# Strassen's method for part of two projections in a float32 encoder kernel on one core

## The chip, the core and the metric

The kernel runs on one core of a Trainium2 chip. Its engines are TensorE (PE in the rows; PEld is its weight load), VectorE (DVE), ScalarE (ACT), GpSimd (POOL) and SyncE (SP), which issues the DMAs. The metric is the device time of one execution in microseconds (us); 2767.62 us is the median of three runs of the kernel before.

## The reference

Two encoder layers on an input of 256 tokens by 2048 columns, in float32. Cut to what the change touches, a layer is:

```python
proj = x @ w_in                      # q, k, v of two attentions, then gate_A and gate_B, 2048 columns each
merged = sigmoid(ga) * (A @ w_pa) + sigmoid(gb) * (B @ w_pb)
x = layer_norm(alpha * x + merged @ w_out)
gate, up = split(x @ w_up)           # w_up is 2048 x 11264, gate and up have 5632 columns each
x = layer_norm(alpha * x + (silu(gate) * up) @ w_down)
```

## The kernel before

**Precision.** Every float32 operand of a large product is split into a high part that TensorE takes exactly and a low rest. ScalarE writes the high part (line 128, L290 for results), VectorE subtracts it to get the low part (L129, L291). A product of two blocks is then three matmuls: high by high (L215), high by low (L216), low by high (L217). All three have a 128 x 128 stationary operand, taken from the turned activations, and 512 moving columns of the weight.

**Tiles.** The 256 tokens are two row tiles t = 0, 1 of 128. The 2048 rows of `w_up` or of a gate are 16 tiles of 128, that is eight pairs. A *piece* is a pair of them by 512 columns (512 KB): one DMA into a `raw` buffer (six of these), one split on ScalarE and VectorE, and 2 row tiles x 2 weight tiles x 3 = 12 matmuls. A *chunk* of `w_up` is 512 gate columns and the 512 up columns that belong to them: eight pieces each, 16 in all, 192 matmuls; there are eleven chunks a layer. A chunk of the gates is 512 columns of gate_A and of gate_B; there are four a layer, each followed by its *merge*, two pieces of `w_pa` and four of `w_pb`.

**Order.** It is written out by hand; each engine runs its instructions in the order of the program. `run()` goes through the pieces. For piece m it first emits the splits up to piece m+3, then the matmuls of m, then what must follow them (`post`), then one item of a list, `background`:

```python
split_to(m + 1 + ahead)
...
pc["mm"](pc)
if pc["post"]:
    pc["post"]()
if background:
    background.pop(0)()
```

So an operation of VectorE that waits for the matmuls of piece m stands behind the splits up to m+3 and ahead of the split of m+4. After a chunk of `w_up`, ScalarE takes silu of the gate accumulator (L748), VectorE multiplies by the up accumulator (L752), and two background items turn the result with four transposes each (L402) and split it (L290, L291). The merge multiplies at L726 and L729 and adds at L730. `ln_turned` puts the loads and products of the layer norm's scale and shift (L436, L437) on the list as well.

**Memory.** An accumulator (`acc`) is two PSUM banks, one for each row tile; there are two, and four single banks (`aux`). Operands lie in 37 `units` of 4 KB a partition. `w_down` is taken in two parts, after chunks 0 to 5 and 6 to 10; the last 512 columns of its second part are done in two halves of 256 columns, for the layer norm that follows.

Of the kernel before, what the change touches and what calls it, by code (L numbers as in the profile page):

```python
# [14 lines left out]
ALU = mybir.AluOpType  # L15
# [61 lines left out]
def trunk(ctx: ExitStack, tc: tile.TileContext, x, rel_bias, w_in, sink, w_pa, w_pb, w_out,  # L77
# [27 lines left out]
    pieces = []  # L105
    background = []
    state = {"load": 0, "split": 0}
    norms = []

    def piece(src, kk, cc, mm, pre=None, post=None):  # L110
        pieces.append(dict(src=src, kk=kk, cc=cc, mm=mm, pre=pre, post=post))
        return pieces[-1]

    def load_to(m):
        while state["load"] < min(m, len(pieces)):
            pc = pieces[state["load"]]
            pc["raw"] = work.tile([P, pc["kk"], pc["cc"]], F32, name="raw", tag="raw", bufs=N_RAW)
            nc.sync.dma_start(pc["raw"], pc["src"])
            state["load"] += 1

    def split_to(m):
        while state["split"] < min(m, len(pieces)):
            load_to(state["split"] + 1 + AHEAD_LOAD)
            pc = pieces[state["split"]]
            raw = pc["raw"]
            hi = unit([P, pc["kk"], pc["cc"]], F32R, "whi")
            lo = unit([P, pc["kk"], pc["cc"]], F32R, "wlo")
            nc.scalar.activation(hi, raw, AF.Copy)  # L128
            nc.vector.tensor_tensor(out=lo, in0=raw, in1=hi.bitcast(F32), op=ALU.subtract)  # L129
            pc["hi"], pc["lo"] = hi, lo  # L130
            state["split"] += 1
# [118 lines left out]
    def gemm_a_halves(w, k0, k1, c0, width, xs, post, between):  # L250
# [398 lines left out]
    def layer(l, xt, pre, turn, after_last):  # L649
# [74 lines left out]
        def merge(c):  # L724
# [123 lines left out]
```

## Time and profile before

| | |
|---|---|
| median of three runs | 2767.62 us |
| the profiled execution | 2767.28 us, of which the span of its instructions is 2765.5 us |
| TensorE busy | 2749.0 us, 99% of the span, 13539 matmuls |
| VectorE busy | 1480.9 us, 54% |
| ScalarE busy | 1168.2 us, 42% |
| DMA | 531.84 MB, mean 192 GB/s |

Busy times of engines overlap one another. A matmul's end is modelled, so consecutive matmuls overlap in the records; how fast TensorE goes is read from the distance of their starts.

### The profile page before, as it was taken

To read this page: it belongs to the slowest core of one execution; us is meant where nothing else is said; L and a number is where in the kernel's file an instruction comes from. 1 tells how busy PE (TensorE), PEld (TensorE's weight loads), DVE (VectorE), ACT (ScalarE), POOL (GpSimd) and SP (SyncE) were. 2 spreads that over 40 slices of the span, in tenths; PEclk is the share of its full clock that TensorE was granted. 3 is DMA by queue.
4 is the path that set the end of the run, shared out by engine and by line. 5 is a ranking of instruction groups with operands and counts; after the bars stand their busy time and mean duration, and the time that the engine had idled before them with its cause. 6 is when DMAs were issued, how large, how long until landed. Compare 5 with 4: busy or idle time off the path is not lost.

```text
span 2765.5 us, 34763 instructions
## 1 busy us (share of the span) xinstructions
PE 2749.0 (99%) x13539; PEld 2319.5 (84%) x13539; DVE 1480.9 (54%) x1688; ACT 1168.2 (42%) x1407; POOL 5.4 (0%) x13
## 2 busy tenths in 40 slices
PE   9999999999999999999999999999999999999998
PEld 7888888888888888888889888888888888888887
DVE  5566554566644544445566655455665444444445
ACT  4454443444333443434344544433544344423441
POOL 0000000000000000000000000000000000000000
PEclk9999999999999999999999999999999999999999
DMA  8866665564655554655656666555645565555554
GB/s 255 241 183 181 185 202 178 187 229 149 225 184 183 208 204 158 211 177 191 215 162 201 179 183 191 177 201 179 232 162 198 183 205 205 183 183 183 187 209 145
DMA packets 359801, 531.84 MB, mean 192 GB/s; under 512 B 52288, under 2 KB 153664, under 8 KB 359636
## 3 DMA queue, kind: packets, MB, share of 16 engines
q1 hardware_dynamic: 358836, 528.31, 58.1%
q8 instruction: 106, 1.74, 0.3%
q10 hardware_dynamic: 800, 1.31, 0.1%
q14 instruction: 59, 0.48, 0.0%
HBM read 522.86 MB, written 6.68 MB: 191 GB/s over the span
## 4 chain that ended last, share of the span: by engine, by line
PE 98%; DVE 1%; DMA 0%; SPq 0%; issue 0%; ACT 0%; DVEq 0%; POOL 0%; ACTq 0%; POOLq 0%
PE acc L217 27%; PE acc L215 27%; PE acc L216 27%; PE acc L202 9%; PE acc L171 5%; PE aux L402 1%; PE aux L297 0%; PE aux L296 0%; PE aux L295 0%; DVE xT L392 0%; PE aux L562 0%; PE aux L528 0%; PE aux L620 0%; PE aux L544 0%; DMA res<-in_x_dram 0%; PE aux L370 0%
## 5 line engine op out<-in xcount | busy, mean ns | idle before, releaser
L129 DVE TENSOR_TENSOR wlo<-raw,whi 128x1024 fp32r<-128x1024 f32 x960 | 1127.4, 1221 | 474.5 <-ACT whi L128 455.4
L128 ACT ACTIVATE whi<-raw 128x1024 fp32r<-128x1024 f32 x960 | 971.5, 1054 | 434.9 <-DMA raw<-in_w_down_dram 142.1
L215 PE MATMUL acc<-whi,xT 128*128 128x512 f32 (+1 forms) x2176 | 848.7, 390 | 0.0
L217 PE MATMUL acc<-whi,xT 128*128 128x512 f32 (+1 forms) x2176 | 842.0, 387 | 0.0
L216 PE MATMUL acc<-wlo,xT 128*128 128x512 f32 (+1 forms) x2176 | 840.8, 386 | 0.0
L217 PEld LDWEIGHTS acc<-whi,xT 128*128 128x128 f32 x2176 | 409.1, 188 | 84.2
L215 PEld LDWEIGHTS acc<-whi,xT 128*128 128x128 f32 x2176 | 409.3, 188 | 80.8 <-issue 0.7
L216 PEld LDWEIGHTS acc<-wlo,xT 128*128 128x128 f32 x2176 | 409.4, 188 | 80.5
L202 PE MATMUL acc<-xT,whi 128*128 128x512 f32 x1088 | 387.0, 399 | 0.0
L171 PE MATMUL acc<-xT,wlo 128*128 128x256 f32 x1088 | 299.6, 280 | 0.0
L215 PE MATMUL acc<-whi,hT 128*128 128x512 f32 (+1 forms) x784 | 288.9, 368 | 0.0
L217 PE MATMUL acc<-whi,hT 128*128 128x512 f32 (+1 forms) x784 | 288.2, 368 | 0.0
L216 PE MATMUL acc<-wlo,hT 128*128 128x512 f32 (+1 forms) x784 | 288.0, 367 | 0.0
L202 PEld LDWEIGHTS acc<-xT,whi 128*128 128x128 f32 x1088 | 203.0, 188 | 43.3
L171 PEld LDWEIGHTS acc<-xT,wlo 128*128 128x128 f32 x1088 | 205.6, 189 | 2.6
L215 PEld LDWEIGHTS acc<-whi,hT 128*128 128x128 f32 x784 | 147.8, 189 | 24.3
L216 PEld LDWEIGHTS acc<-wlo,hT 128*128 128x128 f32 x784 | 147.9, 189 | 24.3
L217 PEld LDWEIGHTS acc<-whi,hT 128*128 128x128 f32 x784 | 147.8, 189 | 24.3
L290 ACT ACTIVATE hT<-aux 128x512 fp32r<-128x512 f32 x44 | 26.3, 598 | 315.2 <-PE aux L402 315.2
L752 DVE TENSOR_TENSOR sg<-sg,acc 128x1024 f32<-128x1024 f32 x22 | 26.9, 1221 | 202.3 <-PE acc L217 202.3
L215 PE MATMUL acc<-whi,mT 128*128 128x512 f32 (+1 forms) x320 | 111.5, 348 | 0.0
L217 PE MATMUL acc<-whi,mT 128*128 128x512 f32 (+1 forms) x320 | 111.0, 347 | 0.0
(133 smaller groups left out, 1503.8 us busy)
## 6 DMA issues: line engine op xcount, KB each, us to landing
raw<-in_w_up_dram SPq DMA_DIRECT2D x352, 512.0 KB, 4.7
raw<-in_w_in_dram SPq DMA_DIRECT2D x320, 512.0 KB, 4.9
raw<-in_w_down_dram SPq DMA_DIRECT2D x176, 512.0 KB, 5.5
raw<-in_w_out_dram SPq DMA_DIRECT2D x64, 512.0 KB, 5.6
raw<-in_w_pb_dram SPq DMA_DIRECT2D x32, 512.0 KB, 5.0
raw<-in_w_pa_dram SPq DMA_DIRECT2D x16, 512.0 KB, 5.9
bias<-ftab SPq DMA_DIRECT2D x96, 64.0 KB, 3.7
ftab<-fb SPq DMA_DIRECT2D x7, 640.0 KB
```

Source lines behind the costliest of these rows:

```text
L128: nc.scalar.activation(hi, raw, AF.Copy)
L129: nc.vector.tensor_tensor(out=lo, in0=raw, in1=hi.bitcast(F32), op=ALU.subtract)
L171: nc.tensor.matmul(st["acc"][:, n, 0:SEQ], lhsT=lo[:, k, n * P:(n + 1) * P], rhs=xs(4 * j + k)[:, 0, :], start=False, stop=False)
L202: nc.tensor.matmul(acc, lhsT=hi[:, k, n * P:(n + 1) * P], rhs=xs(kt).rearrange("p h t -> p (h t)"), start=first and not turn, stop=last)
L215: nc.tensor.matmul(o, lhsT=xk[:, 0, ts], rhs=hi, start=first, stop=False)
L216: nc.tensor.matmul(o, lhsT=xk[:, 0, ts], rhs=lo, start=False, stop=False)
L217: nc.tensor.matmul(o, lhsT=xk[:, 1, ts], rhs=hi, start=False, stop=last)
L290: nc.scalar.activation(hi, src, AF.Copy)
L402: nc.tensor.transpose(out=ps[:, k, t * P:(t + 1) * P], in_=src[:, t, c0:c0 + P], identity=ident)
L752: nc.vector.tensor_tensor(out=s, in0=s, in1=acc, op=ALU.mult)
```

## The change

**Two products at a time.** `gemm_s` computes two column blocks c1 and c2 of 512 (gate and up; or gate_A and gate_B) together. The eight pairs of weight tiles go by `PLAN = "SCSCSCCC"`. A *plain step* C is two pieces, one for each column block, with 24 matmuls as before. A *Strassen step* S takes the same two `raw` tiles (2 weight tiles x 2 column blocks, for 2 row tiles) with seven block products in place of eight, so 21 matmuls, in four pieces, of which the last two load nothing:

- S.1: split of the left tile; products q1 and q2 (6 matmuls)
- S.2: first sum of weight blocks (half of `t13`), split of one block of the right tile (`b22`); product q3 (3)
- S.3: second half of `t13`, first half of `t24`, split of `t13`, second half of `t24`; products q5 and q7 (6)
- S.4: split of `t24`; products q6 and q4 (6)

q2, q3, q4 and x share the two accumulators with the plain steps; q1, q5, q6, q7 take the four `aux` banks. After the third S, `fold()` combines those four into `e` and `f` (one copy on ScalarE, four operations on VectorE). In the last plain step VectorE adds `e` or `f` to each of the four banks as it is finished (L389), and silu, sigmoid and the product then read these sums (L927, L928 for `w_up`).

**Sums of activations.** `sum_rows` makes the sums of activation blocks that the S steps need, for three tiles of two, once for the gates and once for `w_up`, on VectorE with one copy on ScalarE.

**Where.** Chunks 1 to 10 of `w_up` and 1 to 3 of the gates, 26 chunks in both layers; chunk 0 stays as it was and makes room for the sums. Transposes now wait on a list of their own, `soon`, of which S steps and the plain steps up to the one behind the third S take nothing. `w_down` is taken in three parts, after chunks 0 to 3, 4 to 7 and 8 to 10.

```diff
+SUMS = 3
+PLAN = "SCSCSCCC"
...
+    soon = []
...
+            if pc["src"] is not None:
+                pc["raw"] = work.tile([P, pc["kk"], pc["cc"]], F32, name="raw", tag="raw", bufs=N_RAW)
+                nc.sync.dma_start(pc["raw"], pc["src"])
...
+            pc["split"](pc)
...
-            if background:
-                background.pop(0)()
+            if not pc.get("quiet") and (soon or background):
+                (soon or background).pop(0)()
...
+    def gemm_s(w, c1, c2, xs, sums, post, plan=PLAN):
...
+        def bank(n):
+            if "even" not in st:
+                st["even"], st["odd"] = acc_tile(), acc_tile()
+                st.update(q2=st["even"][:, 0, :], q3=st["even"][:, 1, :], q4=st["odd"][:, 0, :], x=st["odd"][:, 1, :])
+            if n not in st:
+                st[n] = aux_tile()
+            return st[n]
...
+            def split2(pc):
+                raw = b["right"] = pc["raw"]
+                b["t13"] = unit([P, 2, 512], F32, "t13")
+                nc.vector.tensor_tensor(out=b["t13"][:, 0, :], in0=b["left"][:, 0, :], in1=raw[:, 0, :], op=ALU.add)
+                b["b22"] = unit([P, 2, 512], F32R, "b22")
+                split_into(b["b22"][:, 0, :], b["b22"][:, 1, :], raw[:, 1, :])
...
+            def split3(pc):
+                b["t24"] = unit([P, 2, 512], F32, "t24")
+                for o, x0, x1 in ((b["t13"][:, 1, :], b["right"][:, 0, :], b["right"][:, 1, :]),
+                                  (b["t24"][:, 0, :], b["t13"][:, 0, :], b["right"][:, 1, :])):
+                    nc.vector.tensor_tensor(out=o, in0=x0, in1=x1, op=ALU.add)
+                b["h13"] = halves(b["t13"])
+                nc.vector.tensor_tensor(out=b["t24"][:, 1, :], in0=b["t24"][:, 0, :], in1=b["left"][:, 1, :], op=ALU.add)
+
+            def split4(pc):
+                b["h24"] = halves(b["t24"])
...
+        def fold():
+
+            e, f, d = unit([P, 2, 512], F32, "e"), unit([P, 2, 512], F32, "f"), work.tile([P, 512], F32, name="tmp", tag="tmp", bufs=2)
+            nc.scalar.activation(e[:, 0, :], st["q1"], AF.Copy)
+            nc.vector.tensor_tensor(out=d, in0=e[:, 0, :], in1=st["q6"], op=ALU.subtract)
+            nc.vector.tensor_tensor(out=e[:, 1, :], in0=d, in1=st["q7"], op=ALU.subtract)
+            nc.vector.scalar_tensor_tensor(f[:, 0, :], st["q5"], -1.0, d, op0=ALU.mult, op1=ALU.subtract)
+            nc.vector.scalar_tensor_tensor(f[:, 1, :], st["q5"], -1.0, e[:, 1, :], op0=ALU.mult, op1=ALU.subtract)
...
+                    if last:
+                        nc.vector.tensor_tensor(out=out_[:, t, :], in0=st[n], in1=st[extra][:, t, :], op=ALU.add)
...
+    def sum_rows(tile_):
...
+        nc.vector.tensor_tensor(out=a.rearrange("p (k t) -> p k t", k=2), in0=tile_[:, :, 0, :].bitcast(F32),
+                                in1=tile_[:, :, 1, :].bitcast(F32), op=ALU.add)
...
+        nc.vector.tensor_tensor(out=d[:, 0:2, :], in0=q[:, 1:4:2, :], in1=q[:, 0:2, :], op=ALU.subtract)
+        nc.vector.tensor_tensor(out=d[:, 2, :], in0=d[:, 1, :], in1=q[:, 0, :], op=ALU.add)
+        nc.vector.tensor_tensor(out=d[:, 3, :], in0=q[:, 2, :], in1=d[:, 2, :], op=ALU.subtract)
+        u = unit([P, 4, 2, P], F32R, "sT")
+        split_into(u[:, :, 0, :], u[:, :, 1, :], d)
...
-        background.extend([lambda: None, lambda: half(0), lambda: half(1)])
+        soon.extend([lambda: None, lambda: half(0), lambda: half(1)])
...
+                pieces[-6]["pre"] = lambda: (flush(), soon.extend([
+                    lambda i=i: xsums.append(sum_rows(xt[i])) for i in range(SUMS)]))
...
+        chunks = ((0, 4), (4, 8), (8, 11))
```

**What moves, first place: VectorE at the end of a chunk of `w_up`.** Before, around the product L752 that ends a chunk (tile numbers are those of the program):

```order
L129 TENSOR_TENSOR wlo_7138<-raw_7045,whi_7137 128x1024 [waits DVE_49,DMAHW0_49,PE_49,Activation_49]
L129 TENSOR_TENSOR wlo_7156<-raw_7063,whi_7155 128x1024 [waits DVE_49,DMAHW1_49,PE_49,Activation_49]
L752 TENSOR_TENSOR sg_7024<-sg_7024,acc_7032 128x1024 [waits PE_49]
L129 TENSOR_TENSOR wlo_7175<-raw_7081,whi_7174 128x1024 [waits DMAHW2_49,DVE_49,Activation_49]
L291 TENSOR_TENSOR hT_7196<-aux_7191,hT_7196 128x2x256 [waits Activation_49]
L129 TENSOR_TENSOR wlo_7202<-raw_7099,whi_7201 128x1024 [waits DMAHW3_49,Activation_49]
L291 TENSOR_TENSOR hT_7222<-aux_7217,hT_7222 128x2x256 [waits Activation_49]
```

Now, from the second half of the transposes of the chunk before, `hT`, to the product L928, where the next chunk begins with an S step too (`acc_8135` holds q2 and q3, `acc_8136` q4 and x):

```order
L443 TENSOR_TENSOR hT_8435<-aux_8430,hT_8435 128x2x256 [waits Activation_49]
L329 TENSOR_TENSOR t13_8440<-raw_8322,raw_8334 128x512 [waits DMAHW0_49]
L443 TENSOR_TENSOR b22_8442<-raw_8334,b22_8442 128x512 [waits Activation_49]
L389 TENSOR_TENSOR sg_8445<-acc_8135,e_8346 128x512 [waits PE_49]
L389 TENSOR_TENSOR sg_8445<-acc_8136,e_8346 128x512 [waits PE_49]
L342 TENSOR_TENSOR t13_8440<-raw_8334 128x512
L342 TENSOR_TENSOR t24_8462<-t13_8440,raw_8334 128x512 [waits DVE_49]
L443 TENSOR_TENSOR tlo_8466<-t13_8440,thi_8465 128x1024 [waits Activation_49]
L344 TENSOR_TENSOR t24_8462<-t24_8462,raw_8322 128x512 [waits DVE_49]
L389 TENSOR_TENSOR sg_8470<-acc_8135,f_8347 128x512 [waits PE_49]
L389 TENSOR_TENSOR sg_8470<-acc_8136,f_8347 128x512 [waits PE_49]
L928 TENSOR_TENSOR sg_8445<-sg_8445,sg_8470 128x1024 [waits DVE_49,Activation_49]
```

One operation that read the accumulator became five, and the sums and splits of the next chunk's S.2 and S.3 stand between them; the split of S.4 follows behind L928.

**Second place: TensorE at the same point.** Before, the first matmul of the next accumulator waited for ScalarE's split and for a release that lay far back:

```order
L215 MATMUL acc_6869<-whi_6954,xT_5502 128x512
L216 MATMUL acc_6869<-wlo_6955,xT_5502 128x512
L217 MATMUL acc_6869<-whi_6954,xT_5502 128x512
L215 MATMUL acc_7032<-whi_6972,xT_5495 128x512 [waits PE_49,Activation_49]
L216 MATMUL acc_7032<-wlo_6973,xT_5495 128x512 [waits DVE_49]
```

Now, from the last plain piece of a chunk to the first products of the next (its accumulator is `acc_8491`):

```order
L304 MATMUL acc_8135<-whi_8388,xT_5664 128x512 [waits DVE_49,Activation_49]
L305 MATMUL acc_8135<-wlo_8389,xT_5664 128x512
...
L304 MATMUL acc_8136<-whi_8388,xT_5664 128x512 [waits DVE_49]
L305 MATMUL acc_8136<-wlo_8389,xT_5664 128x512
...
L304 MATMUL aux_8493<-whi_8414,xT_5657 128x512 [waits Activation_49]
...
L304 MATMUL acc_8491<-whi_8414,xT_5657 128x512 [waits DVE_49]
```

By the counts in the program, the first wait is for VectorE's sum of q2 (the first L389 above), the second for its sum of q4, and the last, that of the next chunk's q2, for the sum of q3 (the third L389), since banks are released by whole tiles.

**Third place: VectorE in the merge of the gates' chunk 0**, from the split of the third-last piece on, before:

```order
L129 TENSOR_TENSOR wlo_3410<-raw_3314,whi_3409 128x1024
L726 TENSOR_TENSOR sg_3194<-sg_3194,acc_3394 128x1024
L129 TENSOR_TENSOR wlo_3429<-raw_3332,whi_3428 128x1024
L129 TENSOR_TENSOR wlo_3448<-raw_3350,whi_3447 128x1024
L129 TENSOR_TENSOR wlo_3466<-raw_3368,whi_3465 128x1024
L129 TENSOR_TENSOR wlo_3484<-raw_3388,whi_3483 128x1024
L729 TENSOR_TENSOR sg_3386<-sg_3386,acc_3432 128x1024
L730 TENSOR_TENSOR sg_3194<-sg_3194,sg_3386 128x1024
```

Now the second of the three `sum_rows` stands behind the product, and the third behind the next split:

```order
L443 TENSOR_TENSOR wlo_3414<-raw_3314,whi_3413 128x1024
L878 TENSOR_TENSOR sg_3194<-sg_3194,acc_3392 128x1024
L417 TENSOR_TENSOR v_3430<-xT_172 128x512
L421 TENSOR_TENSOR v_3430<-v_3430 128x256
L422 TENSOR_TENSOR v_3430<-v_3430 128x128
L423 TENSOR_TENSOR v_3430<-v_3430 128x128
L443 TENSOR_TENSOR sT_3435<-v_3430,sT_3435 128x4x128
L443 TENSOR_TENSOR wlo_3441<-raw_3332,whi_3440 128x1024
L417 TENSOR_TENSOR v_3457<-xT_186 128x512
```

The first `sum_rows` stands ahead of this piece, behind the split of the merge's fourth piece; S.1 to S.3 of the gates' chunk 1 follow the third.

## Rows read from the trace of the kernel before

**Rows 1.** The page, part 1: busy time, share of the span, instructions.

```profile
PE 2749.0 (99%) x13539; PEld 2319.5 (84%) x13539; DVE 1480.9 (54%) x1688; ACT 1168.2 (42%) x1407; POOL 5.4 (0%) x13
```

**Rows 2.** What TensorE waited for: us in total, times, longest.

```profile
PE aux L370 <- DMA res<-in_x_dram: 3.3, 2, 2.3
PE aux L377 <- DVE res L426: 1.5, 3, 0.5
```

**Rows 3.** Timeline of ScalarE (start, us): silu of two consecutive chunks of w_up.

```profile
808.48 1.03 ACT L748 ACTIVATE sg<-acc 128x1024 f32<-128x1024 f32 x1 [10.09 <-PE acc L217]
852.97 1.03 ACT L748 ACTIVATE sg<-acc 128x1024 f32<-128x1024 f32 x1 [10.09 <-PE acc L217]
```

**Rows 4.** Busy times in the 44.49 us between those two.

```profile
808.54:853.03 44.49, 44.49 (x202) 36.81 (x201) 21.13 (x19) 17.72 (x20) 0.00 (x0) 1.00 0.58 189
```

**Rows 5.** Timeline of TensorE: first and last of 22 consecutive matmuls, 512 columns.

```profile
804.65 0.39 PE L217 MATMUL acc<-whi,xT 128*128 128x512 f32 x1
...
809.41 0.39 PE L217 MATMUL acc<-whi,xT 128*128 128x512 f32 x1
```

**Rows 6.** The same: first and last of 19, 256 columns, in w_down.

```profile
2735.83 0.28 PE L217 MATMUL acc<-whi,hT 128*128 128x256 f32 x1
...
2737.99 0.28 PE L217 MATMUL acc<-whi,hT 128*128 128x256 f32 x1
```

**Rows 7.** Timeline of VectorE: runs of operations, 1024 and 512 columns.

```profile
721.50 8.04 DVE L129 TENSOR_TENSOR wlo<-raw,whi 128x1024 fp32r<-128x1024 f32 x7 [0.26 <-ACT whi L128]
...
686.34 0.69 DVE L436 TENSOR_TENSOR res<-res,gb 128x512 f32<-128x512 f32 x1
687.06 0.69 DVE L437 TENSOR_TENSOR res<-res,gb 128x512 f32<-128x512 f32 x1
687.68 2.35 DVE L129 TENSOR_TENSOR wlo<-raw,whi 128x1024 fp32r<-128x1024 f32 x2
```

**Rows 8.** Timeline, hand-overs: VectorE to ScalarE; TensorE, ScalarE, VectorE; VectorE to TensorE.

```profile
169.47 0.69 DVE L680 SCALAR_TENSOR_TENSOR tmp<-acc,tmp 128x512 f32<-128x512 f32 x1 [0.93 <-ACT tmp L281]
170.19 0.63 ACT L290 ACTIVATE parts<-tmp 128x512 fp32r<-128x512 f32 x1 [0.76 <-DVE tmp L680]
...
743.78 0.60 PE L402 MATMUL aux<-ident,sg 128*128 128x128 f32 x4
744.47 0.60 ACT L290 ACTIVATE hT<-aux 128x512 fp32r<-128x512 f32 x1 [12.34 <-PE aux L402]
745.10 0.69 DVE L291 TENSOR_TENSOR hT<-aux,hT 128x512 fp32r<-128x512 f32 x1 [1.49 <-ACT hT L290]
...
654.40 1.45 DVE L426 TENSOR_SCALAR res<-res,mv,rstd 128x512 f32<-128x512 f32 x3
655.09 0.52 PE L377 MATMUL aux<-ident,res 128*128 128x128 f32 x3 [0.49 <-DVE res L426]
```

**Rows 9.** Groups by line and shape: count, busy us, mean ns, idle before.

```profile
L128 ACT ACTIVATE whi<-raw 128x1024 fp32r<-128x1024 f32 x960 | 971.5, 1054 | 434.9 <-DMA raw<-in_w_down_dram 142.1 <-DMA raw<-in_w_up_dram 94.2 <-PE acc L217 66.3
L426 DVE TENSOR_SCALAR res<-res,mv,rstd 128x512 f32<-128x512 f32 x18 | 9.0, 543 | 0.1
L392 DVE TENSOR_TENSOR xT<-v,xT 128x256 fp32r<-128x256 f32 x30 | 12.8, 426 | 1.0
L392 DVE TENSOR_TENSOR xT<-v,xT 128x128 fp32r<-128x128 f32 x12 | 3.5, 292 | 0.4
```

**Rows 10.** Timeline around the merge of a gates' chunk: a split; the merge's end.

```profile
483.99 1.23 DVE L129 TENSOR_TENSOR wlo<-raw,whi 128x1024 fp32r<-128x1024 f32 x1 [11.39 <-ACT whi L128]
...
498.11 0.39 PE L215 MATMUL acc<-whi,xT 128*128 128x512 f32 x1
498.31 1.22 DVE L729 TENSOR_TENSOR sg<-sg,acc 128x1024 f32<-128x1024 f32 x1 [5.12 <-PE acc L217]
```

**Rows 11.** Two stretches near the start, columns as Rows 4; the eighth value is TensorE's granted clock.

```profile
9.00:12.00 3.00, 1.84 (x8) 1.45 (x9) 1.83 (x2) 1.28 (x3) 0.00 (x0) 0.83 1.05 330
12.00:16.00 4.00, 4.00 (x16) 3.20 (x15) 3.05 (x3) 1.91 (x3) 0.00 (x0) 0.70 1.06 286
```

More of the change, by code (lines that the diff above doesn't have):

```diff
@@ L110, in piece @@
     def piece(src, kk, cc, mm, pre=None, post=None):
-        pieces.append(dict(src=src, kk=kk, cc=cc, mm=mm, pre=pre, post=post))
+        pieces.append(dict(src=src, kk=kk, cc=cc, mm=mm, pre=pre, post=post, split=split_plain))
         return pieces[-1]
@@ L116, in load_to, with split_plain @@
             pc = pieces[state["load"]]
-            pc["raw"] = work.tile([P, pc["kk"], pc["cc"]], F32, name="raw", tag="raw", bufs=N_RAW)
-            nc.sync.dma_start(pc["raw"], pc["src"])
+            if pc["src"] is not None:
+                pc["raw"] = work.tile([P, pc["kk"], pc["cc"]], F32, name="raw", tag="raw", bufs=N_RAW)
+                nc.sync.dma_start(pc["raw"], pc["src"])
             state["load"] += 1
+    def split_plain(pc):
+        raw = pc["raw"]
+        pc["hi"] = unit(list(raw.shape), F32R, "whi")
+        pc["lo"] = unit(list(raw.shape), F32R, "wlo")
+        split_into(pc["hi"], pc["lo"], raw)
     def split_to(m):
@@ L124, in split_to @@
             pc = pieces[state["split"]]
[L125 to L130, printed above, removed]
+            pc["split"](pc)
             state["split"] += 1
@@ L733, in merge, with both, post @@
             gemm_a(w_pb[l], 0, 8, 512 * c, 512, lambda kt: lookup(ob)(kt), post_b)
-        for c in range(4):
-            gate(c)
-            merge(c)
+        xsums = []
+        def both(c):
+            def post(a, b):
+                for nm, v in (("a", a), ("b", b)):
+                    nc.scalar.activation(v, v, AF.Sigmoid)
+                    sg[nm] = v
+            gemm_s(wi, GA + 512 * c, GB + 512 * c, xs, xsums, post)
+        for c in range(4):
+            if c == 0:
+                gate(c)
+                merge(c)
+                pieces[-6]["pre"] = lambda: (flush(), soon.extend([
+                    lambda i=i: xsums.append(sum_rows(xt[i])) for i in range(SUMS)]))
+            else:
+                both(c)
+                merge(c)
         stats1 = small.tile([P, 2, 5, 6], F32, name="stats", tag="stats", bufs=2)
@@ L756, in layer, with post_both @@
         after2, between2, ret = after_last(stats2)
-        for half, (c0, c1) in enumerate(((0, 6), (6, 11))):
+        sums = []
+        def post_both(gate_, up_):
+            nc.scalar.activation(gate_, gate_, AF.Silu)
+            nc.vector.tensor_tensor(out=gate_, in0=gate_, in1=up_, op=ALU.mult)
+            turn_block(gate_, hs, "hT")
+        chunks = ((0, 4), (4, 8), (8, 11))
+        for part, (c0, c1) in enumerate(chunks):
             for c in range(c0, c1):
                 st = {}
-                gemm_a(w_up[l], 0, KT, 512 * c, 512, x1s, lambda acc, st=st: post_gate(acc, st),
-                       turn=(turn1 if c == 0 else None))
+                if c > 0:
+                    gemm_s(w_up[l], 512 * c, D_FF + 512 * c, x1s, sums, post_both)
+                    continue
+                gemm_a(w_up[l], 0, KT, 512 * c, 512, x1s, lambda acc, st=st: post_gate(acc, st), turn=turn1)
                 gemm_a(w_up[l], 0, KT, D_FF + 512 * c, 512, x1s, lambda acc, st=st: post_up(acc, st))
-            residual_gemm(w_down[l], 4 * c0, 4 * c1, lookup(hs), ALPHA if half == 0 else None,
-                          None if half == 0 else stats2, after2, between2)
+                pieces[-12]["pre"] = lambda: background.__setitem__(slice(0, 0), [
+                    lambda i=i: sums.append(sum_rows(x1t[i])) for i in range(SUMS)])
+            last = part == len(chunks) - 1
+            residual_gemm(w_down[l], 4 * c0, 4 * c1, lookup(hs), ALPHA if part == 0 else None,
+                          stats2 if last else None, after2, between2)
         if l < DEPTH - 1:
```

77 lines of the change are left out of this document (added).

## The prediction

> **What bounds the kernel now.** I began with busy times. TensorE is busy 99% of the span, VectorE 54%, ScalarE 42% [rows 1], and the view of waits gives TensorE 4.8 us in all [rows 2]. So the time is the number of matmuls by their spacing. In TensorE's timeline 22 matmuls of 512 columns start within 4.76 us, hence 4.76 / 21 = 0.2267 us each [rows 5]; those of 256 columns take 2.16 / 18 = 0.120 us [rows 6]. A chunk of `w_up` lasts 44.49 us from silu to silu [rows 3]: 192 x 0.2267 = 43.52, and 0.97 for two groups of transposes (0.485 each). In that window VectorE works 21.13 us, ScalarE 17.72, and the granted clock is 1.00, the 2.4 GHz level [rows 4]. A matmul taken out is time gained, as long as VectorE can prepare operands at the new pace.
>
> **What is removed.** Each S step does 21 matmuls for 24, three S a chunk: 9 fewer in 26 chunks (10 of `w_up` and 3 of the gates in each layer), 234 x 0.2267 = 53.05 us. The last columns of `w_down` lose 192 matmuls of 256 columns for 96 of 512: 23.04 - 21.76 = 1.28. Together 54.3 us, 2.04 a chunk. The point that decides is thus 54.3 / 26 = 2.09 us of new waiting a chunk.
>
> **What is added on VectorE.** The prices: seven 1024-column operations in 8.04 us, the last of them 1.22 long, start (8.04 - 1.22) / 6 = 1.137 apart; independent ones of 512 columns start 0.62 apart (687.06 to 687.68; I use 0.61), 0.72 where the second reads the first's result (686.34 to 687.06) [rows 7]. An S step has three low parts of 1024, one of 512 and four sums of 512. Two of the low parts can't begin until a sum has gone to ScalarE and back: 0.69 for the sum, 0.03 to hand over (169.47 + 0.69 to 170.19 [rows 8]), 1.05 for the copy [rows 9], about 0.03 back (an estimate, from 744.47 + 0.60 to 745.10 [rows 8]), 1.81 us from a sum's start to its low part's. The longest path through an S and a C step on this engine is five spacings of 1024 (t24's low part, two of C, the next left tile, t13's low part), two of 512 and two round trips: 5 x 1.137 + 2 x 0.61 + 2 x 1.81 = 10.52 us. TensorE needs 45 x 0.2267 = 10.20 for the same. So VectorE falls 0.32 behind with each S-C pair, if it begins without a lead.
>
> **The end of a chunk that another S follows.** The order in the first place of the change puts sums between splits. I laid it out from zero = the last matmul of the fourth plain step. Transposes of the second half: TensorE's 0.485; their low part on VectorE 1.32 after their start (743.78 to 745.10 [rows 8]), say 1.33. From there by spacings: half of t13 1.94, b22 2.55, sum of q2 3.16 (ends 3.85), sum of q4 3.77, second half of t13 4.38, its low part 4.38 + 1.81 = 6.19, second half of t24 7.33, sum of q3 7.94 (ends 8.63), sum of x 8.55, L928 9.27, low part of t24 10.41 (ends 11.63). VectorE to TensorE takes 0.15 (654.94 to 655.09 [rows 8]). TensorE: the left last piece ends at 0.485 + 12 x 0.2267 = 3.21; the right one has to wait for the sum of q2 until 4.00 (**0.79**); it ends at 6.72, q1 at 7.40; q2 of the next chunk waits for the sum of q3 until 8.78 (**1.38**); S.2 and S.3 follow, and S.4 waits for the low part of t24 until 11.78 (**0.05**). Second and third S each lose the **0.32** (0.33) above. Sum 2.87 us, against 2.04 saved: such a chunk takes 42.46 + 2.87 = 45.33. There are seven such boundaries a layer (1-2, 2-3, 4-5, 5-6, 6-7, 8-9, 9-10): 14 x 2.87 = 40.2.
>
> **Other places.** The other 12 chunks end before a plain step or a merge: low part 1.33, a split 1.94, sum of q2 3.08, end 3.77 + 0.15, wait 0.71: 8.5 in all. In the six chunks of gates the second and third S lose 0.65 each chunk: 3.9; two entries behind a merge a layer 0.33 each: 1.3. Chunks of `w_up` behind `w_down` or chunk 0 come in with a lead, as VectorE has 2 x 1.137 = 2.3 of work for 5.4 us of a plain step: nothing. The loads and products of the layer norm stand between two chunks: 1.33 x 2 = 2.7.
>
> `sum_rows` in the merge: a sum of 512, 256 and two of 128 columns and a low part, in series, with two copies on ScalarE: about 3.45 us each (from 0.69, 0.426, 0.292 and 0.60 [rows 8, 9] with their hand-overs; an estimate). Three of them with five splits, the product L878 and the sums and low parts of S.1 to S.3 make a chain of 24.4 us on VectorE from the split that starts at 483.99. In the trace the last products of that merge begin at 498.11 [rows 10]; the S step's q1 would begin after 15 more matmuls (3.40) and needs its operands at 501.7. VectorE is there at 508.4 + 0.15: a wait of 6.8, 2 x 6.8 = 13.6. Hidden I take the third part of `w_down` (four more updates of the residual a layer: in those stretches VectorE has the 3 us of room a step named above; uncovered they would cost 8 x 0.69 = 5.5) and the DMAs (same number; six buffers of `raw` are a lead of some 11 us at 12 x 0.2267 = 2.72 us a piece, less where pieces load nothing).
>
> **Sum.** 40.2 + 8.5 + 3.9 + 1.3 + 2.7 + 13.6 = 70.2 us of waiting, less 54.3: +15.9. The profiled execution took 2767.28 (its median stands 0.34 above): **2783 us**, 0.6% slower.
>
> Bounds for the unknowns. The spacing of 512 columns on VectorE: 0.61 to 0.72 [rows 7]; were all sums 0.72, each boundary costs 8 x 0.11 = 0.9 more, +12. Hand-overs may be shorter than I allow: without the last one to TensorE (0.15) and the twelve of 0.03 in three S steps, a chunk loses 0.5 less, 14 x 0.5 = -7. `sum_rows`: 2.3 (spacings alone) to 3.9 each, -7 to +3. I take the middle values, since these rows are of the same operations.
>
> **A rule to weigh.** Rows 7 show an operation starting before the one ahead has ended (1.137 apart, 1.22 long). The Trainium skill, "VectorE: DVE Perf Modes", section "The DRAIN you can't avoid", says that the next operation does not start until the pipe is empty; the trace disagrees for this kernel's splits, and the page itself excepts operations that are not held. Rows 7 decide my sum. By the page's rule it would be the third rival's.
>
> **Rivals.**
>
> *VectorE keeps ahead and TensorE hardly waits* (the other side). Its mechanism: the lead. The splits stand four pieces ahead, 10.9 us of matmuls; if the plain steps C4 and C5 rebuild more than the 0.32 + 2.2 that a boundary spends, the sums don't come late. With no waits 2767.3 - 54.3 = 2713; with half of the 70.2, 2748. For it: 21.13 of 44.49 us busy [rows 4], some 42 afterwards (20 operations of 1.22, 25 of 0.69), still under the chunk. Against: the sum of q2 stands behind low parts that wait for transposes, whatever the lead. It decides under 2.09 us a chunk. Chance 0.05 for all, 0.17 for a gain that is partly kept (2725 to 2762).
>
> *The waits eat the gain and no more*: 1.1 less at each boundary (spacings of 0.55 would do it), 14 x 1.1 = 15.4, hence 2768. Chance 0.17.
>
> *VectorE's operations do not overlap where they differ from one another*: durations of 1.22 and 0.69 as spacings. The S-C path gets 5 x 0.083 + 2 x 0.08 = 0.58 longer, a boundary 0.9: 2.05 a chunk of `w_up`, 28.7; 3.5 + 3.5 for gates, 2.4 for `sum_rows`, 2 for the others: +40, **2823**. Rows 7 speak against it. Chance 0.06.
>
> *The clock falls.* After 3.3 us of waits at 9 to 10.5 us TensorE was granted 0.83, then 0.70 of full speed [rows 11]: 3.0 x 0.17 + 4.0 x 0.30 = 1.7 us lost. If the two waits of a boundary (2.2 us within 5) do it as well, 14 boundaries and three entries of the gates make 17 x 1.7 = 29: **2812**. Chance 0.10. The Trainium skill, "TensorE: Matmul & The Clock Gate", section "HAM oscillation — how this bites in real kernels", tells of kernels whose clock falls again and again with gaps in TensorE's work; rows 11 show one such fall, and no row here shows one in a stretch of short waits.
>
> **Numbers.** My forecast holds 0.45, between 2773 and 2798. A measurement of this kernel can tell about 0.2%, 5.5 us. Faster 0.22, same 0.17, slower 0.45 + 0.06 + 0.10 = 0.61. Range: leaving out 2823, 2713 and the lower half of the partial gain (0.06 + 0.05 + 0.08) gives 2748 to 2815.
>
> **What would show it.** The profile after should have TensorE's waits near 75 us, on VectorE: L389 at the ends of chunks, L443 `tlo` in S.4; silus of consecutive chunks 45.3 apart (42.5 without waits); a gap of about 7 us before the gates' chunk 1; matmuls 0.227 apart and a granted clock of 1.00 between. I am wrong if silus stand under 44.5 apart, if the waits name ScalarE or a DMA, or if the clock falls.

## The result

The changed kernel takes 2805.97 us (median of four runs, 2805.58 to 2806.83) against 2767.91 us for the kernel before on the same chips: a ratio of 1.014 with a 95% interval from 1.0127 to 1.0152. It is 38 us slower; the forecast was 16 us. The sign and the engine were right, the size was not.

The page of the kernel after, part 1 (compare [rows 1]):

```profile
PE 2728.2 (97%) x13209; PEld 2261.4 (81%) x13209; DVE 1973.7 (70%) x2432; ACT 1306.2 (47%) x1601; POOL 5.4 (0%) x13
```

What TensorE waited for in it (compare [rows 2]; columns: us in total, times, longest):

```profile
PE acc L304 <- DVE sg L389: 34.9, 36, 2.3
PE aux L305 <- DVE tlo L443: 10.3, 25, 1.9
PE aux L304 <- ACT thi L442: 2.9, 6, 0.9
```

TensorE has 330 matmuls fewer and waits for VectorE in the two places that were named: for the sums L389 at the end of a chunk, and for the low part `tlo` in S.4. No DMA stands among the new waits. ScalarE stands there with 2.9 us, and what it waits for is a sum of VectorE.

A chunk with an S chunk before and behind it, between two silus in ScalarE's timeline:

```profile
1020.22 1.04 ACT L927 ACTIVATE sg<-sg 128x1024 f32<-128x1024 f32 x1
1065.86 1.04 ACT L927 ACTIVATE sg<-sg 128x1024 f32<-128x1024 f32 x1
```

Busy times in that stretch (columns as in [rows 4]):

```profile
1020.22:1065.86 45.64, 43.83 (x193) 34.81 (x192) 38.62 (x45) 22.87 (x27) 0.00 (x0) 1.00 0.60 185
```

It takes 45.64 us, where it was 44.49 before [rows 3] and would be 42.46 without waits. VectorE is busy for 38.62 of these 45.64 us, so its busy time has room; the granted clock is 1.00. The stalls of this chunk stand in TensorE's timeline:

```profile
1017.18 0.39 PE L306 MATMUL acc<-whi,xT 128*128 128x512 f32 x1
1018.17 0.47 PE L304 MATMUL acc<-whi,xT 128*128 128x512 f32 x1 [0.60 <-DVE sg L389]
...
1021.46 0.39 PE L306 MATMUL aux<-whi,xT 128*128 128x512 f32 x1
1022.83 0.50 PE L304 MATMUL acc<-whi,xT 128*128 128x512 f32 x1 [0.98 <-DVE sg L389]
...
1036.00 0.39 PE L304 MATMUL aux<-thi,sT 128*128 128x512 f32 x1
1036.53 0.50 PE L305 MATMUL aux<-tlo,sT 128*128 128x512 f32 x1
1036.87 0.40 PE L306 MATMUL aux<-thi,sT 128*128 128x512 f32 x1
```

A stall is read from the distance of the starts, less 0.2267: the right last piece waits 0.99 - 0.23 = 0.76 for the sum of q2; q2 of the next chunk 1.37 - 0.23 = 1.14 for the sum of q3; S.4 0.53 - 0.23 = 0.30, and the matmul behind it starts 0.11 late too. The number in brackets is smaller by 0.16, since a matmul's modelled end lies 0.39 behind its start; the third stall has no bracket at all. So the view of waits, 58.8 us in all, tells too little: the span grew from 2765.5 to 2803.8 us, and 38.3 us more with 54.3 us of matmuls gone make 92.6 us of new stalls.

On VectorE, the operations of one S step and the C step behind it, in the same chunk:

```profile
1024.62 1.22 DVE L443 TENSOR_TENSOR tlo<-t,thi 128x1024 fp32r<-128x1024 f32 x1
1025.76 3.49 DVE L443 TENSOR_TENSOR wlo<-raw,whi 128x1024 fp32r<-128x1024 f32 x3
1029.16 0.69 DVE L329 TENSOR_TENSOR t<-raw 128x512 f32<-128x512 f32 x1
1029.77 0.69 DVE L443 TENSOR_TENSOR b<-raw,b 128x512 fp32r<-128x512 f32 x1
1030.37 0.69 DVE L342 TENSOR_TENSOR t<-raw 128x512 f32<-128x512 f32 x1
1030.97 0.69 DVE L342 TENSOR_TENSOR t<-t,raw 128x512 f32<-128x512 f32 x1
1032.24 1.23 DVE L443 TENSOR_TENSOR tlo<-t,thi 128x1024 fp32r<-128x1024 f32 x1 [0.58 <-ACT thi L442]
1033.38 0.68 DVE L344 TENSOR_TENSOR t<-t,raw 128x512 f32<-128x512 f32 x1
1035.25 1.22 DVE L443 TENSOR_TENSOR tlo<-t,thi 128x1024 fp32r<-128x1024 f32 x1 [1.19 <-ACT thi L442]
```

From t24's low part to the next one's: 35.25 - 24.62 = 10.63 us, and TensorE needs 10.20. The two round trips are 1030.37 to 1032.24 and 1033.38 to 1035.25, 1.87 each; VectorE sits idle in them for 0.58 and 1.19 us (the brackets).

### The profile page after: what moved, and what is told of

It is laid out like the page before. It is cut to its first block, busy times and chain, and to the rows that moved or that the text cites. A ratio compares the mean times of both kernels' runs of the same rounds, so it can differ in the third digit from the quotient of the medians.

```text
span 2803.8 us, 34938 instructions
## 1 busy us (share of the span) xinstructions
PE 2728.2 (97%) x13209; PEld 2261.4 (81%) x13209; DVE 1973.7 (70%) x2432; ACT 1306.2 (47%) x1601; POOL 5.4 (0%) x13
## 4 chain that ended last, share of the span: by engine, by line
PE 73%; DVE 16%; ACT 5%; issue 4%; DMA 1%; SPq 0%; DVEq 0%; ACTq 0%; POOL 0%; POOLq 0%
PE acc L220 12%; PE acc L222 12%; PE acc L221 12%; PE acc L207 9%; PE acc L304 6%; PE acc L306 6%; PE acc L305 6%; DVE wlo L443 5%; PE acc L176 5%; ACT thi L442 3%; DVE tlo L443 3%; DVE sg L389 1%; PE aux L305 1%; DVE t L344 1%; DVE t L342 1%
## 5 line engine op out<-in xcount | busy, mean ns | idle before, releaser
L443 DVE TENSOR_TENSOR wlo<-raw,whi 128x1024 fp32r<-128x1024 f32 x882 | 1036.8, 1220 | 121.5 <-ACT whi L442 119.9
L442 ACT ACTIVATE whi<-raw 128x1024 fp32r<-128x1024 f32 x882 | 890.4, 1051 | 261.5 <-DMA raw<-in_w_down_dram 108.9
L304 PE MATMUL acc<-whi,xT 128*128 128x512 f32 x1118 | 443.1, 396 | 34.9 <-DVE sg L389 34.9
L306 PE MATMUL acc<-whi,xT 128*128 128x512 f32 x1118 | 436.3, 390 | 0.0
L305 PE MATMUL acc<-wlo,xT 128*128 128x512 f32 x1118 | 435.6, 390 | 0.0
L442 ACT ACTIVATE thi<-t 128x1024 fp32r<-128x1024 f32 x156 | 165.5, 1061 | 501.2 <-DVE t L342 317.7
L304 PEld LDWEIGHTS acc<-whi,xT 128*128 128x128 f32 x1118 | 209.9, 188 | 91.1 <-DVE sg L389 25.1
L443 DVE TENSOR_TENSOR tlo<-t,thi 128x1024 fp32r<-128x1024 f32 x156 | 191.0, 1225 | 108.2 <-ACT thi L442 108.2
L306 PEld LDWEIGHTS acc<-whi,xT 128*128 128x128 f32 x1118 | 209.8, 188 | 45.1
L305 PEld LDWEIGHTS acc<-wlo,xT 128*128 128x128 f32 x1118 | 210.1, 188 | 41.9
L220 PE MATMUL acc<-whi,xT 128*128 128x512 f32 (+1 forms) x512 | 195.9, 383 | 0.9 <-ACT xT L442 0.9
L221 PE MATMUL acc<-wlo,xT 128*128 128x512 f32 (+1 forms) x512 | 193.2, 377 | 1.0 <-DVE wlo L443 1.0
L222 PE MATMUL acc<-whi,xT 128*128 128x512 f32 (+1 forms) x512 | 193.1, 377 | 0.6 <-DVE xT L443 0.6
```

The lines of the kernel that those rows point to most:

```text
L220: nc.tensor.matmul(o, lhsT=xk[:, 0, ts], rhs=hi, start=first, stop=False)
L221: nc.tensor.matmul(o, lhsT=xk[:, 0, ts], rhs=lo, start=False, stop=False)
L222: nc.tensor.matmul(o, lhsT=xk[:, 1, ts], rhs=hi, start=False, stop=last)
L304: nc.tensor.matmul(o, lhsT=xk[0], rhs=hi, start=first, stop=False)
L305: nc.tensor.matmul(o, lhsT=xk[0], rhs=lo, start=False, stop=False)
L306: nc.tensor.matmul(o, lhsT=xk[1], rhs=hi, start=False, stop=last)
```

## The experiments

Theory: TensorE waits because of the *order* of VectorE's operations (two round trips in series, sums behind them), not for want of room on the engine. Rivals: release of banks by whole tiles; waits that follow the method wherever its steps stand; stalls that the profile only makes up. All runs are compared with the kernel before on the same chip (2766.9 to 2768.0 us).

**One round trip in place of two (e1).** In S.3:

```diff
-                b["h13"] = halves(b["t13"])
                 nc.vector.tensor_tensor(out=b["t24"][:, 1, :], in0=b["t24"][:, 0, :], in1=b["left"][:, 1, :], op=ALU.add)
+                b["h13"] = halves(b["t13"])
```

> The second half of t24 is summed ahead of the split of t13, so an S step has one round trip through ScalarE on VectorE's path in place of two; the work is the same. Theory (TensorE waits because VectorE's order puts two round trips in series, 10.64 us for an S and a C step against 10.20 on TensorE): the pair falls to 10.64 - 1.87 = 8.8 us, the stalls of S.4 (0.42 each, some 55 of them) go, the sum of q3 comes about 0.6 earlier at the end of a chunk; 35 to 40 us less, about 2769. Rival (the waits come from banks released by whole tiles, or from DMA): the same stalls come back under another name, 2800 to 2806.

Measured: 2778.52 us, 1.0035 [1.0022, 1.0048] of before, 27 us less than the changed kernel. VectorE's timeline of that run:

```profile
1022.39 0.68 DVE L342 TENSOR_TENSOR t<-raw 128x512 f32<-128x512 f32 x1
1022.99 0.68 DVE L342 TENSOR_TENSOR t<-t,raw 128x512 f32<-128x512 f32 x1
1023.71 0.69 DVE L343 TENSOR_TENSOR t<-t,raw 128x512 f32<-128x512 f32 x1
1024.32 2.49 DVE L443 TENSOR_TENSOR tlo<-t,thi 128x1024 fp32r<-128x1024 f32 x2
1026.73 3.49 DVE L443 TENSOR_TENSOR wlo<-raw,whi 128x1024 fp32r<-128x1024 f32 x3
```

Both low parts now follow one another without idle time, and a pair takes 8.95 us (1024.32 to 1033.27, where the next pair's two stand). TensorE's stalls for a low part `tlo` in S.3 and S.4 fell from 55 to 12, eight of these at the entries behind the sums of activations, and a chunk went from 45.64 us to 44.1 or 44.2. The theory holds for the S steps. The expected 37 us were not reached: the eight stalls at the entries stayed, 8.0 us together, and the waits at the chunk's end are still 0.7 to 1.0 for the sum of q2 and 0.65 to 1.2 for that of q3 (2.0 where the layer norm's products stand).

**Another sharing of the accumulators (e2).** `q2` and `q4` in the one, `q3` and `x` in the other:

```diff
-                st.update(q2=st["even"][:, 0, :], q3=st["even"][:, 1, :], q4=st["odd"][:, 0, :], x=st["odd"][:, 1, :])
+                st.update(q2=st["even"][:, 0, :], q4=st["even"][:, 1, :], q3=st["odd"][:, 0, :], x=st["odd"][:, 1, :])
```

> The two accumulators are shared out anew: q2 and q4 in one, q3 and x in the other, so the last plain piece and q2 of the next chunk wait for no sum of the piece in hand. Theory (VectorE's order is the bound): between two chunks with S steps the wait only moves to q3, behind the sum of x, and nothing is won there; the 12 other chunk ends win about 1.0 each: 2806 - 12 = 2794. Rival (release by whole tiles is the cause of the chunk-end stalls, 0.7 to 1.0 and 1.1 to 1.8 us each): 26 x 0.85 + 14 x 1.25 = 40 us less, 2766.

Measured: 2923.54 us, 1.056 [1.0544, 1.0576]. Neither expectation held. The sum of q2 is taken between the matmuls of q2 and of q4 of the same piece; with both in one tile q4 now waits for a sum of its own piece. TensorE's timeline shows it between the two, and again a piece later between q3 and x:

```profile
1097.22 0.40 PE L306 MATMUL acc<-whi,xT 128*128 128x512 f32 x1
1099.44 0.50 PE L304 MATMUL acc<-whi,xT 128*128 128x512 f32 x1 [1.82 <-DVE sg L389]
...
1102.07 0.39 PE L306 MATMUL acc<-whi,xT 128*128 128x512 f32 x1
1106.03 0.80 PE L304 MATMUL acc<-whi,xT 128*128 128x512 f32 x1 [3.57 <-DVE sg L389]
1106.62 0.63 PE L305 MATMUL acc<-wlo,xT 128*128 128x512 f32 x1
1107.05 0.63 PE L306 MATMUL acc<-whi,xT 128*128 128x512 f32 x1
```

The run shows that waits on a whole tile are real, and that the edit was made at half its length: the sums have to move behind the piece's last matmul too (done in e6). Behind the longer wait the matmuls start 0.43 apart, at the lower clock; the mean granted clock of this run is 0.976. Some 250 of its matmuls stand so, in 26 stretches, each 0.20 late, 50 us of TensorE's time; how much of the 118 us over the changed kernel is the clock's and how much the waits', no run takes apart.

**Sums of activations split a piece later (e3).** `sum_rows` returns the sums, and the list holds its parts apart:

```diff
+        return [lambda: adds(0), lambda: (low(0), adds(1)), lambda: (low(1), adds(2)), lambda: low(2)]
...
-                    lambda i=i: xsums.append(sum_rows(xt[i])) for i in range(SUMS)]))
```

> Each sum of activations is split one piece later than it is summed, so that ScalarE's copy and the split of the next piece no longer wait in turn for VectorE. Theory (the three sums with their round trip cost 4.65 us of VectorE a piece and so the 6.5 us stall ahead of the gates' chunk 1 and the 3 us stall in chunks 0 and 1 of w_up): the two stalls fall to some 2 and 1 us a layer, 13 us less in all, about 2793. Rival (the stall is the room in memory or the start of S.1 to S.3 themselves): 2803 to 2806.

Measured: 2791.61 us, 1.0084 [1.0067, 1.0101], 14 less than the changed kernel, as expected. The stalls ahead of and in the first S step of the gates fell from 6.8 to 3.5 us a layer; those of chunk 0 and of the first S step behind it, some 3 us a layer, went. The edit does one thing more: it takes four places of the list in place of three, so that one of two pairs of the layer norm's products moves out of that S step to the end of the chunk (VectorE, second pair at 745.57 us, in the changed kernel at 703.21). What went in chunk 1 is therefore not shown to be the sums' alone.

**w_down in three parts alone (e4)**, in the kernel before:

```diff
-        for half, (c0, c1) in enumerate(((0, 6), (6, 11))):
+        for part, (c0, c1) in enumerate(((0, 4), (4, 8), (8, 11))):
```

> The kernel before with w_down in three parts alone. Matmuls: -1.28 us; the end behind the last matmul 2.3 us longer, as in the kernel after (13.0 against 10.6): together +1.0, 2769. Rival (the four more updates of the residual a layer are not hidden): 8 x 0.69 = 5.5 more, 2774.

Measured: 2768.84 us, 1.0003 [0.9994, 1.0012]. The updates of the residual are hidden; the expected +1.0 lies within what can be told.

**A plain step first (e5).** PLAN `CSCSCSCC`; both halves of the turn stand behind the first plain step, and plain steps between S steps take from `background`.

```diff
-PLAN = "SCSCSCCC"
+PLAN = "CSCSCSCC"
...
-        soon.extend([lambda: None, lambda: half(0), lambda: half(1)])
+        soon.extend([lambda: None, lambda: None, lambda: (half(0), half(1))])
```

> The same steps in another order, PLAN CSCSCSCC in place of SCSCSCCC; both halves of the turn are done behind the first plain step. Theory (VectorE's order): with a plain step first the sums of q3 and x stand behind plain splits and no round trip, so the wait of q2 for the sum of q3 goes, and the lead of that step takes up what the S steps lose; but all of VectorE's path in a chunk, three pairs of 10.64, four splits of 1.137, fold, sums and turn, 43.9 us, is then the bound where another S chunk follows: 1.5 of loss in place of 3.2. About 45 us less in all, 2761. Rival (room is there on VectorE, only the order is wrong): chunks at 42.5 + 0.7, 2740. Other rival (the waits follow the S steps wherever they stand): 2800 to 2806.

Measured: 2779.9 us, 1.0047 [1.0032, 1.0062]; 26 less, where the theory had 45 and the second rival 66. Chunks that follow one another take 43.5 us, close to the 43.9 that VectorE's path gives. The gates won 0.7 us a chunk, and the chunk with the layer norm's products stayed at 46.7. One wait, at the end of chunk 1, is 3.1 us long (TensorE's timeline):

```profile
745.68 0.39 PE L308 MATMUL acc<-whi,xT 128*128 128x512 f32 x1
749.16 0.47 PE L306 MATMUL acc<-whi,xT 128*128 128x512 f32 x1 [3.09 <-DVE sg L391]
```

Windows behind it (columns as in [rows 4], the granted clock the eighth value):

```profile
749.20:753.10 3.90, 3.90 (x11) 3.03 (x12) 2.23 (x3) 1.58 (x2) 0.00 (x0) 0.57 0.49 160
753.10:757.00 3.90, 3.90 (x19) 3.22 (x18) 3.12 (x5) 0.00 (x0) 0.00 (x0) 0.99 0.02 4
```

The granted clock was 0.57 of full speed for 3.9 us. Order alone, with two round trips kept, does not make the kernel faster than before.

**All together (e6).** e1, e3, e5, e2 with the sums behind the piece's last matmul, and `w_down` in parts of 4, 3 and 4 chunks:

```diff
+                if last:
+                    for t, n in enumerate(names_):
                         nc.vector.tensor_tensor(out=out_[:, t, :], in0=st[n], in1=st[extra][:, t, :], op=ALU.add)
...
-        chunks = ((0, 4), (4, 8), (8, 11))
+        chunks = ((0, 4), (4, 7), (7, 11))
```

> Four edits together: t24 summed first, sums of activations split a piece later, plain step first, q2 and q4 in one accumulator with both sums taken behind the piece's last matmul; w_down in parts of 4, 3 and 4 chunks, so that the end is as before. Theory (VectorE's path per chunk falls to 38.3 us, below TensorE's 42.46, and no sum is waited for at a chunk's end): the 54 us of matmuls are won, less some 4 us a layer around the first gates and 3 us of small waits: about 2724. Rival (the saving is lost in the method itself, by slower matmuls or an engine that is full): not under 2755.

Measured: 2720.14 us, 0.9833 [0.9818, 0.9847]: faster than both kernels, 47 us below before and 86 below the changed kernel, with the same products, sums and splits in these chunks (in `w_down` its parts take 48 matmuls more). Two silus of that run in ScalarE's timeline:

```profile
1184.63 1.06 ACT L942 ACTIVATE sg<-sg 128x1024 f32<-128x1024 f32 x1 [8.03 <-DVE sg L392]
1227.00 1.06 ACT L942 ACTIVATE sg<-sg 128x1024 f32<-128x1024 f32 x1 [8.03 <-DVE sg L392]
```

The window between them:

```profile
1184.69:1227.06 42.37, 42.37 (x192) 35.17 (x191) 38.63 (x46) 22.78 (x27) 0.00 (x0) 1.00 0.59 198
```

VectorE is busy for 38.63 us and ScalarE for 22.78, as in the changed kernel (38.62 and 22.87), and yet the chunk takes 42.37 us instead of 45.64. VectorE's work is the same; what differs is its order and the sharing of the accumulators, which is 11 us of the whole (e11). VectorE's idle time ahead of the low parts of the sums went from 108.2 us (changed kernel) to 2.9, and TensorE's longest kind of wait for a sum from 34.9 us to 3.9.

**The gates as before (e7)**, so that only `w_up` goes by sums (each turn of the loop over c is `gate(c)` and `merge(c)` again).

> The changed kernel with the gates computed as before, so that only w_up is done by sums. Theory, from the stalls of the trace after: the gates save 6 x 2.04 = 12.2 us and lose 6 x 2.25 + 2 x 6.5 = 26.5; without them 14 us less, 2792. Rival (stalls that show in the trace are partly the profile's): a change under 6 us.

Measured: 2790.64 us, 1.0086 [1.0071, 1.0101], 15 less. The stalls read in the trace are real time.

**One sum twice (e8)**: t24's second half is summed twice in each S step.

> The changed kernel with one sum of 512 columns on VectorE done twice in each S step, 78 more operations of 0.69 us. Theory (VectorE's order sets the pace of the S steps): each of them moves the end by its spacing, 78 x 0.6 = 47 us, 2853; at most the six that begin with a lead are hidden. Rival (VectorE is 70% busy and the stalls are hand-overs of banks and buffers): mostly hidden, 2806 to 2815.

Measured: 2855.44 us, 1.0318 [1.0301, 1.0335]: 49 us for 78 operations, 0.63 each. An engine that is busy 70% of the time hid none of them.

**Each part taken out of e6.** e9 has t24 in the order of the changed kernel, e10 has the S step first, e11 has the accumulators shared as in the changed kernel; the later split of the sums and the parts of `w_down` were not taken out. e12 adds a fourth S step, PLAN `CSCSCSSC`.

> All the edits together, but t24 summed behind the split of t13 as in the changed kernel. Theory (one round trip more in each S step, 1.87 us, makes VectorE's path of a chunk 43.9 us against 42.4 on TensorE): chunks that follow one another go from 42.4 to 43.5, the gates lose about 0.5 a chunk: 14 x 1.1 + 6 x 0.5 = 18 us more than all edits together, 2738. Rival (with a plain step first the lead hides the second round trip): 2720 to 2724.

Measured: 2753.27 us, 0.9946 [0.9931, 0.9961], 33 more than e6. Chunks that follow one another take 43.4 us, as expected; the rest is that the others pay as well (gates 1.0 us a chunk, chunk 1 of `w_up` 2.2, the one with the layer norm's products 2.6), since a path longer than TensorE's leaves no lead to build up.

> All the edits together, but the S step first as in the changed kernel. Theory (the sums of q3 and x stand behind S.3 of the next chunk): q3 of S.2 waits for the sum of x, which ends 8.7 us after the fourth plain step, while TensorE is there at 7.3: 1.6 us at 14 boundaries, 22 us more than all together, 2742. Rival (the accumulators' new sharing alone frees TensorE): 2720 to 2726.

Measured: 2763.4 us, 0.9981 [0.9972, 0.9991], 43 more. The wait of q3 for the sum of x is 1.8 us at twelve boundaries, where I had 1.6; it is 3.1 at the end of each layer's chunk 1 and 2.8 behind each layer's first merge, which I had not counted. These waits come to 33 of the 43 us; the rest is not taken apart.

> All the edits together, but the accumulators shared as in the changed kernel, q2 with q3 and q4 with x. Theory (the right last piece waits for the sum of q2, since a bank is released with the other bank of its tile): 0.7 us a chunk, 26 x 0.7 = 18 us more than all together, 2738. Rival (that wait is taken up by the lead elsewhere): 2720 to 2724.

Measured: 2731.08 us, 0.9868 [0.9853, 0.9883], 11 more, less than the theory's 18. Where chunks follow one another they take 42.5 us: VectorE is early enough there that the sum of q2 is hardly waited for. The longest waits left stand at the end of chunk 1, 3.9 and 3.8 us, where e6 has 1.4 and 0.8 in each layer. So release by whole tiles is the smallest of the three parts. With the later split of the sums, 14 us by itself (e3), the parts come to more than the 86 us between the changed kernel and e6, so they overlap.

> All the edits together with four S steps in eight, CSCSCSSC: three matmuls fewer again in each of 26 chunks, 17.7 us. Theory (VectorE's path decides): four pairs of 8.95, as in the run with t24 first, and 7.4 for fold, sums, product and turn make 43.2 us against 41.8 on TensorE, so nothing is won and about 0.8 a chunk is lost where S chunks follow one another: 2725 to 2735. Rival (VectorE has room): 2703.

Measured: 2747.18 us, 0.9924 [0.991, 0.9939], 27 more than e6 and above the 2725 to 2735 of the theory. Chunks that follow one another take 43.1 to 43.2 us, as VectorE's path says; chunk ends ahead of `w_down` and of a merge lose more; fold stands right ahead of the last step there, which I take for the reason without a run that shows it. Three S steps are what VectorE feeds in this order.

## Why the prediction was right in sign and short in size

The removed work was right: 330 matmuls, 54.3 us. The stalls come to 92.6 us where I had 70.2. The mechanism was right; two terms that I had put at nothing were 7.8 and 2.3 us, and three were too small by 4 to 5 us each. By places, from TensorE's starts and the stages' lengths:

| term | forecast | measured |
|---|---|---|
| 14 chunk ends with an S chunk behind | 40.2 | 44.7 (3.19 each) |
| layer norm's products | 2.7 | 2.6 |
| the 6 other ends of `w_up` chunks | 4.3 | 8.4 |
| gates: ends and S steps of 6 chunks | 9.5 | 14.0 |
| sums ahead of the gates' chunk 1 | 13.6 | 13.1 |
| sums in chunk 0 of `w_up`, and chunk 1 | 0 | 7.8 |
| the end behind the last matmul | 0 | 2.3 |

- **The S-C path on VectorE** was right in kind (e1, e8, e9) and 0.11 short a pair, 10.63 for 10.52: a round trip takes 1.87, not 1.81 (its terms add up to 1.80). The second and third S step of a chunk so lose 0.42 each (0.31 and the late matmul behind it, 0.11) where I had 0.32 and 0.33. That is 0.19 of the 0.32 by which the first row's chunks differ; 0.17 is small lengthenings of the other distances, and the chunk's end is a little shorter than forecast.
- **The sums at a chunk's end** were right: 0.70 to 0.76 (none behind chunks 4 and 8) and 1.14 to 1.79, 2.47 with the layer norm's products, where I had 0.79 and 1.38. At the other ends I had 0.71 and measured 0.98 to 1.04 and 0.08 for the matmul behind. There the split ahead of the sum waits for ScalarE's copy, and the sum starts that much later. Behind chunk 3 the first product of `w_down` waits 0.9 as well: a pair of the layer norm's products stands ahead of that sum, which I had not looked at. The gates' row has the same causes: 1.06 at each end for 0.71, and mostly 0.35 to 0.46 in each S step of the second and third S chunk.
- **`sum_rows`** ahead of the gates was right to 0.5 us in its sum, but not in its place. The row at 498.11 [rows 10] is the first product of the next chunk (`xT`), not of the merge, and 15 matmuls behind it stands q6 of S.4, not q1. Up to there the waits do add up to 6.8 us; they come as six, 0.5 to 2.2 us each, from S.1 to S.4, and no gap of 7 us stands ahead of the chunk.
- **The step that failed** is "chunks of `w_up` behind `w_down` or chunk 0 come in with a lead ... nothing". For chunks 4 and 8 it holds (no stall in the trace). Behind chunk 0 it fails, with 7.8 us in both layers. In chunk 0 stand the same three `sum_rows`, 4.65 us each with the split behind, for 2.72 us of matmuls a piece: 1.0 us of stalls a layer. They stand ahead of the layer norm's load and products in the list, and push them into chunk 1's first S step. There VectorE, with the splits done, waits for the DMA of the layer norm's scale before it comes to the first sum, and TensorE loses 2.9 us in the first layer's chunk 1 and 2.5 in the second's (the rest of the 7.8 is small lengthenings, below). I had priced the sums and the products in one place each. Which of the two costs how much in chunk 1 stays open, since e3 moves both. VectorE's timeline of the changed kernel:

```profile
690.28 6.90 DVE L443 TENSOR_TENSOR wlo<-raw,whi 128x1024 fp32r<-128x1024 f32 x6 [2.06 <-ACT whi L442]
700.64 0.69 DVE L588 TENSOR_TENSOR res<-res,gb 128x512 f32<-128x512 f32 x1 [3.46 <-DMA gb<-in_ln_g_dram]
...
702.01 0.68 DVE L329 TENSOR_TENSOR t<-raw 128x512 f32<-128x512 f32 x1
```

- **w_down in three parts** I took as hidden. Its updates are (e4). But the last part has 12 weight tiles in place of 20, so TensorE's second half at the end lasts 4.3 us, and VectorE needs 6.6 for the first half's layer norm. The end behind the last matmul grew from 10.6 to 13.0 us, more than the 1.28 us won.

```profile
2786.55 0.42 DVE L596 TENSOR_TENSOR res<-res,acc 128x256 f32<-128x256 f32 x1 [2.85 <-PE acc L222]
...
2790.55 0.28 PE L222 MATMUL acc<-whi,hT 128*128 128x256 f32 x1
...
2791.84 1.41 DVE L965 SCALAR_TENSOR_TENSOR res<-res,rstd,gb 128x512 f32<-128x512 f32 x2
2793.16 0.41 DVE L596 TENSOR_TENSOR res<-res,acc 128x256 f32<-128x256 f32 x1
```

These rows are VectorE's, with TensorE's last matmul among them: the second update (2793.16) no longer waits for TensorE, which was done at 2790.6 + 0.3, but for the engine itself.

**The rivals.** The lead did not save it: a busy share under the chunk's length was true (38.62 of 45.64) and meant nothing, as e8 shows. VectorE's operations overlap as [rows 7] had them: three of 1024 columns in 3.49 us are 1.135 apart, so the rule of the Trainium skill ("VectorE: DVE Perf Modes", "The DRAIN you can't avoid"), that the next operation waits until the pipe is empty, does not hold for them; the section itself excepts operations that are not held. The clock stayed at 1.00 through stalls of up to 2.5 us in the profiled execution of the changed kernel, so that rival was wrong for it, but by no margin that the runs show: in e3 the clock fell behind a wait of the same kind and length, one chunk earlier (below).

Not settled: some 4 us of the 92 lie in small lengthenings of matmul distances (those under 0.28 average 0.2275 us, before 0.2271), which no run here takes apart.

## What to carry to other kernels

Before a matmul is replaced by sums on another engine, lay out that engine's operations in program order with the spacing of each and with every round trip through a third engine, and compare this path, not the busy share, with the matmuls' time: here 38.6 us of work fitted into 42.4 in one order and took 45.6 in another. Put independent operations into a round trip, and put sums that free an accumulator where no round trip stands ahead of them. Price a burst at each place where it occurs, and read stalls from the distance of starts, since modelled ends hide the short ones.

## What the hardware showed beside

- After a stall TensorE's second matmul is late as well: its start stands 0.34 behind the first's instead of 0.23 (1036.53 to 1036.87), in nearly every stall of the changed kernel.
- Behind a wait of 3.1 us in e5 and of 3.6 us in e2 the matmuls stood 0.43 apart (1106.62 to 1107.05), the 1.2 GHz level, and in e5 the granted clock was back at 0.99 after 3.9 us. In e5 it fell to 0.51 behind waits of 0.5, 0.8 and 2.0 us ahead of the gates' chunk 1 too. In the changed kernel six waits stand at that place, 5.1 us together and the longest 1.9, and the clock stays at 1.00. The longest wait of that kernel, 2.31 us for the sum of q3 at the end of chunk 2, where a pair of the layer norm's products stands ahead of it, did not lower it either. In e3 that pair stands at the end of chunk 1, and there a wait of the same 2.31 us did lower it, in both layers (TensorE's timeline, first the changed kernel, then e3):

```profile
800.22 0.50 PE L304 MATMUL acc<-whi,xT 128*128 128x512 f32 x1 [2.31 <-DVE sg L389]
800.78 0.40 PE L306 MATMUL acc<-whi,xT 128*128 128x512 f32 x1
...
751.19 0.57 PE L304 MATMUL acc<-whi,xT 128*128 128x512 f32 x1 [2.31 <-DVE sg L389]
751.99 0.63 PE L306 MATMUL acc<-whi,xT 128*128 128x512 f32 x1
752.42 0.63 PE L304 MATMUL acc<-b,sT 128*128 128x512 f32 x1
```

The window behind it in e3 (the granted clock is the eighth value):

```profile
751.20:755.00 3.80, 3.80 (x10) 2.99 (x11) 3.70 (x4) 3.79 (x5) 0.00 (x0) 0.55 0.46 144
```

So the length of a wait alone does not tell here whether the clock falls. The Trainium skill, "TensorE: Matmul & The Clock Gate", "HAM oscillation — how this bites in real kernels", tells of gaps that lower the clock again and again; e2, e3 and e5 agree. In e5 each such fall made 7 to 12 matmuls 0.20 late, 1.4 to 2.4 us of TensorE's time. That need not reach the end: in e8 a chunk with such a fall took 47.82 us from silu to silu and one without it 47.81, since TensorE waits for VectorE in both.
